# One column block of the output projection: the weights' low parts come from an adding DMA instead of a VectorE subtraction

## The chip, the cores and the metric

The kernel runs on one core of a Trainium2 chip. The core has five engines that work side by side, each through its own queue, in order: TensorE (PE in the profile; PEld is its weight load), VectorE (DVE), ScalarE (ACT), GpSimd (POOL) and SyncE (SP). Sixteen DMA engines move data between the chip's memory (HBM), where inputs and outputs lie, and the on-chip memory. A DMA is started by an instruction in the queue of SP, ACT or POOL. The metric is the device time of one execution in microseconds (us), smaller is better. Before the change it is 1098.4 us (median of three runs, 1097.79 to 1098.97).

## The reference

One layer of a decoder trunk on 512 tokens of width 2048. The change touches the output projection, the third line here:

```python
h = rms_norm(x, norm_g[i])
z = jnp.einsum('btd,dn->btn', h, w_in[i])        # then two head groups, gated, give y_mix
x = x + jnp.einsum('btc,cd->btd', y_mix, w_out[i])
gate = jax.nn.sigmoid(jnp.einsum('btd,de->bte', x, w_pg[i]) + b_pg[i])
x = x + gate * jnp.einsum('btq,qd->btd', p[i], w_ple[i])
return rms_norm(x, final_g)
```

`y_mix` is 512 x 2048 and `w_out` 2048 x 2048, all float32.

## The kernel before, in words

TensorE multiplies in the type float32r, which keeps fewer bits than float32. To keep the precision each operand is split into a high part (the value cast to float32r) and a low part (the value less the high part, cast too), and each product is made of three: high by high, high by low, low by high. `mm3` (L164) issues these three matmuls into one PSUM tile.

The program runs in stages: the input projection with the recurrence over the heads beside it (to about 728 us), the output projection (728 to 909 us), the gate projection and the final norm. The output projection goes through four column blocks of 512 columns, `ec` = 0 to 3 (loop at L987). In a block `proj` (L940) goes through 16 chunks of 128 rows of `w_out`, in the order 8 to 13, 0 to 7, 14, 15 (`order`). A chunk is a tile of 128 x 512 float32, 256 KB. For each chunk, and each of the four token tiles `tt`, `mm3` runs once: 12 matmuls of 128x512 a chunk, into four accumulators `acc_o`. The first matmul of a token tile reads `whi`, the second `wlo`, the third `whi` again (with `ylo`).

A chunk is prepared by `wsplit` (L127):

```python
raw = wp.tile([P, kt, n], F32, name=f"raw_{nm}", tag="raw")
nc.sync.dma_start(out=raw, in_=src)
hi = wp.tile([P, kt, n], F32R, name=f"whi_{nm}", tag="whi")
lo = wp.tile([P, kt, n], F32R, name=f"wlo_{nm}", tag="wlo")
nc.scalar.copy(hi, raw)
nc.vector.tensor_tensor(lo, raw, hi.bitcast(F32), ALU.subtract)
```

So SP starts the load of `raw`, ACT casts it to `whi` (L132), DVE subtracts to `wlo` (L133). The tags `raw`, `whi` and `wlo` have four buffers each (`wp`, `bufs=4`). ACT can cast a chunk only when TensorE has done with the chunk four places before it, whose buffer it takes; the loads run further ahead.

At the end of a block DVE adds `x` to each accumulator (L995), ACT's queue starts a store of the sum to `x2d` (L996) and later a load of the next block's `x` (L994). TensorE transposes the sums in 16 pieces of 128 x 128 (L1002) into four tiles `px`, each of which ACT casts to `x2hi` and DVE splits to `x2lo` (L137, L138). The framework's scheduler sets the order of the instructions on each engine from its own estimate of their times; no order is written out by hand in this stage. POOL has no work in the stage, and no instruction in the whole program that starts a DMA.

Of the kernel before, what the change touches and what calls it, by code (L numbers as in the profile page):

```python
# [9 lines left out]
F32 = mybir.dt.float32  # L10
F32R = mybir.dt.float32r
I32 = mybir.dt.int32
AF = mybir.ActivationFunctionType
ALU = mybir.AluOpType

P = 128
# [18 lines left out]
def trunk_kernel(ctx: ExitStack, tc: tile.TileContext, x, p, norm_g, w_in, mu, w0, w_up, a0, a_up,  # L35
                 k_k, k_a, r_k, ln_w, ln_b, w_pool, pool_scale, w_out, w_ple, w_pg, b_pg, final_g, out):
    nc = tc.nc
    PSUM = bass.MemoryType.PSUM
    x, p, w_in, w_out, w_ple, w_pg = x[0], p[0, 0], w_in[0], w_out[0], w_ple[0], w_pg[0]
    out = out[0]  # L40
# [3 lines left out]
    wp = ctx.enter_context(tc.tile_pool(name="wp", bufs=4))  # L44
# [82 lines left out]
    def wsplit(src, kt, n, nm):  # L127
# [6 lines that stand above are left out]
        return hi, lo  # L134

    def split(hi, lo, src):
        c_ = nc.scalar.copy(hi, src)  # L137
        nc.vector.tensor_tensor(lo, src, hi.bitcast(F32), ALU.subtract)  # L138
        return c_
# [24 lines left out]
    def mm3(ps, wh, wl, xh, xl, first, last):  # L164
        mm(ps, wh, xh, start=first, stop=False)
        mm(ps, wh, xl, start=False, stop=False)
        return mm(ps, wl, xh, start=False, stop=last)
# [8 lines left out]
    def chunk(nm, c, ahead=2):  # L176
        while (nm, c) not in ready or ahead > 0:
            if (nm, c) in ready:
                ahead -= 1
            if not plan:  # L180
                break
            n_, c_, src, kt, w_ = plan.pop(0)
            if (n_, c_) not in ready:
                ready[n_, c_] = wsplit(src, kt, w_, f"{n_}_{c_}")
        return ready.pop((nm, c))
# [8 lines left out]
    EC = 512  # L194
# [101 lines left out]
    for d in range(KT):  # L296
        xt_half(0, d)
        if d in WPOS:
            c = len(wl_)
            wh = wp.tile([P, CK, P], F32R, name=f"whi_l_{c}", tag="whi")  # L300
            wl = wp.tile([P, CK, P], F32R, name=f"wlo_l_{c}", tag="wlo")
# [586 lines left out]
    for j in range(NJ):  # L888
# [6 lines left out]
        if j + 1 == NJ:  # L895
            pn.append(rw.tile([P, NT, DPLE], F32, name="pn", tag="ar", bufs=2))
            for h in range(2):
                nc.scalar.dma_start(out=pn[0][:, 2 * h:2 * h + 2, :],
                                    in_=p[256 * h:256 * h + 256, :].rearrange("(t p) q -> p t q", p=P))
# [16 lines left out]
    def load_y(k):  # L916
        t_ = ymp.tile([P, T], F32, name=f"yin{k}", tag="yin", bufs=AHEAD)
        nc.scalar.dma_start(out=t_, in_=yd[k])
        split(yhi[:, k, :], ylo[:, k, :], t_)
# [15 lines left out]
    def acc_tile(nm):  # L935
        nacc[0] += 1
        pool, tag = (psB, "accb") if nacc[0] % 5 in (1, 2, 3) else (psA, "acc")
        return pool.tile([P, EC], F32, name=nm, tag=tag)

    def proj(w, hi_, lo_, ec, nm, ks=range(KT), tts=range(NT), keep=None, aside=None):  # L940
        acc = {tt: acc_tile(f"acc_{nm}{ec}_{tt}") for tt in tts}
        for i, k in enumerate(ks):
            src = w[k * P:(k + 1) * P, ec * EC:(ec + 1) * EC].unsqueeze(1)
            if nm == "o" and ec == 0 and i + AHEAD < KT:
                load_y(ks[i + AHEAD])
            if (f"{nm}{ec}_{k}", 0) in ready:
                wh, wl = ready.pop((f"{nm}{ec}_{k}", 0))
            elif nm == "o" and ec == 0 and i < 4:
                wh, wl = chunk(f"{nm}{ec}_{k}", 0)
            elif keep is None or LATE <= i < KT - KEEP:  # L950
                wh, wl = wsplit(src, 1, EC, f"{nm}{ec}_{k}")
            else:
                raw = wp.tile([P, 1, EC], F32, name=f"raw_{nm}{ec}_{k}", tag="raw")
                nc.sync.dma_start(out=raw, in_=src)
                if i < 2:
                    if i == 0:
                        two = [pp.tile([P, 2, EC], F32R, name=f"{g}k", tag=g, bufs=1) for g in ("dh", "dl")]
                    wh, wl = (g[:, i:i + 1, :] for g in two)
                else:
                    own = i < KT - 4  # L960
                    wh, wl = ((kp_ if own else wp).tile([P, 1, EC], F32R, name=f"{g}k{k}",
                                                        tag=f"{g}k{k}" if own else g) for g in ("whi", "wlo"))
                split(wh, wl, raw)
                keep[k] = (wh, wl)
                if i >= LATE:
                    continue
            for tt in tts if keep is None or i >= LATE else tts[:-1]:
                ts_ = slice(tt * P, (tt + 1) * P)
                first = i == (LATE if keep is not None and tt == NT - 1 else 0)
                e_ = mm3(acc[tt], hi_[:, k, ts_], lo_[:, k, ts_], wh[:, 0, :], wl[:, 0, :], first, i == KT - 1)  # L970
            if aside is not None and i == 2:
                with tc.issue_after(e_.ins):
                    hi = aside()
                with tc.issue_after(hi.ins):
                    recall(0, lp)
        return acc
# [3 lines left out]
    def recall(ec, pool):  # L980
        ples[ec] = []
        for tt in range(NT):
            t_ = pool.tile([P, EC], F32, name=f"pler{ec}_{tt}", tag="ple", bufs=4)
            nc.scalar.dma_start(out=t_, in_=pled[tt * P:(tt + 1) * P, ec * EC:(ec + 1) * EC])
            ples[ec].append(t_)

    for ec in range(D // EC):  # L987
        es = slice(ec * EC, (ec + 1) * EC)
        acc = proj(w_out, yhi, ylo, ec, "o", order)
        x2 = []  # L990
        for tt in range(NT):
            rows = slice(tt * P, (tt + 1) * P)
            t_ = pp.tile([P, EC], F32, name=f"x2_{ec}_{tt}", tag=("u", "sw")[tt // 2])
            nc.scalar.dma_start(out=t_, in_=x[rows, es])  # L994
            nc.vector.tensor_tensor(t_, acc[tt], t_, ALU.add)  # L995
            nc.scalar.dma_start(out=x2d[rows, es], in_=t_)  # L996
            x2.append(t_)
        def turn(ec=ec, x2=x2):
            for i in range(EC // P):
                pt = psM.tile([P, T], F32, name=f"px2_{ec}_{i}", tag="m")  # L1000
                for tt in range(NT):
                    nc.tensor.transpose(pt[:, tt * P:(tt + 1) * P], x2[tt][:, i * P:(i + 1) * P], ident)  # L1002
                hi = split(x2hi[:, 4 * ec + i, :], x2lo[:, 4 * ec + i, :], pt)
            return hi


        if ec < D // EC - 1:
            turn()
# [4 lines left out]
    with tc.tile_pool(name="fp", bufs=2) as fp, tc.tile_pool(name="kp_", bufs=1) as kp_:  # L1013
# [92 lines left out]
        for ec in range(LAST):  # L1106
            pre = {}
            vec = vectors(ec)
            acc = proj(w_pg, x2hi, x2lo, ec, "g", aside=turn if ec == 0 else None)
            ple = ples.pop(ec)  # L1110
            recall(ec + 1, fp if ec % 2 == 0 else lp)
            for tt in range(NT):
                fetch(ec, tt)
                gate(acc[tt], ec, tt, slice(ec * EC, (ec + 1) * EC), ec)
        ec = LAST
# [3 lines left out]
        for tt in range(NT):  # L1119
            fetch(ec, tt)  # L1120
        acc = proj(w_pg, x2hi, x2lo, ec, "g", keep=kept)


# [57 lines left out]
```

## Time and profile before

| | |
|---|---|
| median of three runs | 1098.4 us (1097.79 to 1098.97) |
| profiled execution | 1097.72 us |
| its span, first to last instruction | 1095.9 us |
| mean granted TensorE clock | 0.998 |
| second column block of the output projection | 772.57 to 817.99 us: 45.42 us |
| third column block | 817.99 to 863.44 us: 45.45 us |

The span is what the profiler saw between the first and the last instruction; the device time is 1.8 us longer. A timeline row gives the start, the duration, the engine, the line, the tiles written and read, and in brackets how long the engine had idled and for whom. ACTq and SPq rows are the instructions with which a queue starts DMAs, not the transfers. Matmuls overlap in the pipeline, so the distance between starts is the pace, and the duration is not. A strip of DMA digits shows the busy share of the 16 DMA engines in tenths, in 40 equal slices of the stretch asked for.

### The profile page before, as it was taken

To read this page: it belongs to the slowest core of one execution; us is meant where nothing else is said; L and a number is where in the kernel's file an instruction comes from. 1 tells how busy PE (TensorE), PEld (TensorE's weight loads), DVE (VectorE), ACT (ScalarE), POOL (GpSimd) and SP (SyncE) were. 2 spreads that over 40 slices of the span, in tenths; PEclk is the share of its full clock that TensorE was granted. 3 is DMA by queue.
4 is the path that set the end of the run, shared out by engine and by line. 5 is a ranking of instruction groups with operands and counts; after the bars stand their busy time and mean duration, and the time that the engine had idled before them with its cause. 6 is when DMAs were issued, how large, how long until landed. Compare 5 with 4: busy or idle time off the path is not lost.

```text
span 1095.9 us, 17196 instructions
## 1 busy us (share of the span) xinstructions
PE 1070.8 (98%) x6060; PEld 877.6 (80%) x6060; DVE 708.2 (65%) x1835; ACT 448.3 (41%) x917; POOL 76.9 (7%) x180
## 2 busy tenths in 40 slices
PE   5999999999999999999999999999999999999996
PEld 4888878887788888788878788888888888888885
DVE  6687867878688679678886956454433424445366
ACT  7633535345335335353343344543222222233337
POOL 2100110110110110100101101000000000000000
PEclk9999999999999999999999999999999999999999
DMA  7433433332423333333334242775534438455534
GB/s 233 116 96 97 111 92 84 96 100 73 120 82 105 104 92 89 96 82 93 91 94 119 79 138 93 232 233 169 172 124 136 167 99 244 137 189 137 181 106 154
DMA packets 178486, 138.56 MB, mean 126 GB/s; under 512 B 34678, under 2 KB 139743, under 8 KB 178399
## 3 DMA queue, kind: packets, MB, share of 16 engines
q1 hardware_dynamic: 157694, 103.89, 32.1%
q10 hardware_dynamic: 20704, 33.56, 9.8%
q8 instruction: 48, 0.79, 0.3%
q14 instruction: 40, 0.32, 0.1%
HBM read 118.02 MB, written 18.87 MB: 125 GB/s over the span
## 4 chain that ended last, share of the span: by engine, by line
PE 86%; DVE 5%; DMA 4%; ACT 3%; issue 1%; SPq 0%; ACTq 0%; DVEq 0%
PE acc_o L157 16%; PE zb L157 14%; PE acc_g L157 14%; PE zv L157 8%; PE zk L157 7%; PE zg L157 7%; PE zr L157 7%; PE py L157 2%; PE pple L157 2%; PE pm L157 1%; PE pu L157 1%; DMA n<-nd 1%; PE pp L157 1%; DMA raw_g<-in_w_pg_dram 1%; PE ps L157 1%
## 5 line engine op out<-in xcount | busy, mean ns | idle before, releaser
L133 DVE TENSOR_TENSOR wlo_g<-raw_g,whi_g 128x512 fp32r<-128x512 f32 x84 | 57.0, 685 | 79.6 <-ACT whi_g L132 76.5
L157 PE MATMUL zb<-hhi,whi_b 128*128 128x512 f32 x256 | 107.0, 418 | 0.0
L133 DVE TENSOR_TENSOR wlo_o<-raw_o,whi_o 128x512 fp32r<-128x512 f32 x64 | 43.9, 690 | 91.4 <-ACT whi_o L132 91.4
L157 PE MATMUL zb<-hhi,wlo_b 128*128 128x512 f32 x256 | 100.5, 393 | 0.0
L157 PE MATMUL acc_o<-whi_o,ylo 128*128 128x512 f32 x256 | 100.2, 391 | 0.0
L157 PE MATMUL acc_o<-whi_o,yhi 128*128 128x512 f32 x256 | 99.9, 390 | 0.0
L157 PE MATMUL zb<-hlo,whi_b 128*128 128x512 f32 x256 | 99.9, 390 | 0.0
L157 PE MATMUL acc_o<-wlo_o,yhi 128*128 128x512 f32 x256 | 99.8, 390 | 0.0
L132 ACT CAST whi_g<-raw_g 128x512 fp32r<-128x512 f32 x84 | 51.9, 620 | 102.7 <-PE acc_g L157 55.4
L157 PE MATMUL acc_g<-whi_g,x2hi 128*128 128x512 f32 x208 | 81.3, 391 | 0.0
L157 PE MATMUL acc_g<-wlo_g,x2hi 128*128 128x512 f32 x208 | 80.9, 389 | 0.0
L157 PE MATMUL acc_g<-whi_g,x2lo 128*128 128x512 f32 x208 | 80.7, 389 | 0.0
L132 ACT CAST whi_o<-raw_o 128x512 fp32r<-128x512 f32 x64 | 39.9, 623 | 97.0 <-PE acc_o L157 96.7
L816 POOL TENSOR_SCALAR s0p<-sbd,pw 64x64 f32<-64x64 f32 x96 | 56.6, 589 | 322.8 <-DVE sbd L809 255.0
L132 ACT CAST whi_b<-raw_b 128x512 fp32r<-128x512 f32 x64 | 39.7, 621 | 86.5 <-PE zv L157 35.4
L133 DVE TENSOR_TENSOR wlo_b<-raw_b,whi_b 128x512 fp32r<-128x512 f32 x64 | 43.8, 685 | 34.2 <-ACT whi_b L132 32.9
L157 PEld LDWEIGHTS zb<-hhi,wlo_b 128*128 128x128 f32 x256 | 48.0, 188 | 11.1
L661 DVE TENSOR_TENSOR xw<-xw,tm 128x60 f32<-128x60 f32 (+24 forms) x248 | 52.1, 210 | 6.8
L157 PEld LDWEIGHTS acc_o<-wlo_o,yhi 128*128 128x128 f32 x256 | 48.1, 188 | 10.3 <-DVE wlo_o L133 0.4
L157 PEld LDWEIGHTS acc_o<-whi_o,yhi 128*128 128x128 f32 x256 | 48.1, 188 | 9.7
L157 PEld LDWEIGHTS acc_o<-whi_o,ylo 128*128 128x128 f32 x256 | 48.1, 188 | 9.8
L157 PEld LDWEIGHTS zb<-hhi,whi_b 128*128 128x128 f32 x256 | 48.2, 188 | 8.5
(285 smaller groups left out, 2550.0 us busy)
## 6 DMA issues: line engine op xcount, KB each, us to landing
raw_b<-in_w_in_dram SPq DMA_DIRECT2D x64, 256.0 KB
raw_o<-in_w_out_dram SPq DMA_DIRECT2D x64, 256.0 KB
raw_g<-in_w_pg_dram SPq DMA_DIRECT2D x64, 256.0 KB
raw_k<-in_w_in_dram SPq DMA_DIRECT2D x32, 256.0 KB
raw_r<-in_w_in_dram SPq DMA_DIRECT2D x32, 256.0 KB
raw_v<-in_w_in_dram SPq DMA_DIRECT2D x32, 256.0 KB
raw_g<-in_w_in_dram SPq DMA_DIRECT2D x32, 256.0 KB
n<-nd SPq DMA_DIRECT2D x16, 256.0 KB
```

What stands on the lines that cost most here:

```text
L132: nc.scalar.copy(hi, raw)
L133: nc.vector.tensor_tensor(lo, raw, hi.bitcast(F32), ALU.subtract)
L157: i = nc.tensor.matmul(*a, **k)
L661: nc.vector.tensor_tensor(xw[:, 0:n_, s + 1:32], xw[:, 0:n_, s + 1:32], tm[:, 0:n_, 0:w_], ALU.add)
L816: nc.gpsimd.tensor_scalar(s0p[hc, :], nxt[hc, hc], pcn[hc], None, ALU.mult)
```

## The change

In the second column block alone (`ec == 1`, all 16 chunks) the chunk is prepared in another way. SP still loads `raw` and ACT still casts it to `whi`. Then ACT writes the negated high part to `wlo`, and a DMA in POOL's queue reads the same piece of `w_out` from HBM a second time and adds it onto `wlo`. DVE has no part in it.

```diff
@@ -947,6 +947,14 @@
             elif nm == "o" and ec == 0 and i < 4:
                 wh, wl = chunk(f"{nm}{ec}_{k}", 0)
+            elif nm == "o" and ec == 1:
+                raw = wp.tile([P, 1, EC], F32, name=f"raw_{nm}{ec}_{k}", tag="raw")
+                nc.sync.dma_start(out=raw, in_=src)
+                wh = wp.tile([P, 1, EC], F32R, name=f"whi_{nm}{ec}_{k}", tag="whi")
+                wl = wp.tile([P, 1, EC], F32R, name=f"wlo_{nm}{ec}_{k}", tag="wlo")
+                nc.scalar.copy(wh, raw)
+                nc.scalar.activation(wl, wh.bitcast(F32), AF.Copy, scale=-1.0)
+                nc.gpsimd.dma_start(out=wl, in_=src, accum_op=ALU.add)
             elif keep is None or LATE <= i < KT - KEEP:
                 wh, wl = wsplit(src, 1, EC, f"{nm}{ec}_{k}")
```

DVE loses 16 instructions, ACT gains 16 and POOL gains 16. Lines after L949 move down by 8, so the transposes of L1002 stand at L1010 in the rows of the changed kernel. The scheduler also orders TensorE's and ACT's instructions otherwise at the seam of the first and the second block.

On TensorE, at the seam before the change: `px_0_i` is the transpose of the first block's column piece i, `x_0_tt` the sum of token tile tt, `acc_o_0_8485` the second block's first accumulator.

```order
L1002 MATMUL px_0_0_8457<-ident,x_0_2_8449 128x128
L1002 MATMUL px_0_1_8464<-ident,x_0_2_8449 128x128
L1002 MATMUL px_0_2_8471<-ident,x_0_2_8449 128x128
L157 MATMUL acc_o_0_8485<-whi_o_8_8491,yhi 128x512
L157 MATMUL acc_o_0_8485<-wlo_o_8_8492,yhi 128x512
L1002 MATMUL px_0_0_8457<-ident,x_0_3_8453 128x128
L1002 MATMUL px_0_1_8464<-ident,x_0_3_8453 128x128
L1002 MATMUL px_0_2_8471<-ident,x_0_3_8453 128x128
L157 MATMUL acc_o_0_8485<-whi_o_8_8491,ylo 128x512
```

The same place on TensorE in the changed kernel:

```order
L1010 MATMUL px_0_2_8471<-ident,x_0_0_8441 128x128
L1010 MATMUL px_0_2_8471<-ident,x_0_1_8445 128x128
L1010 MATMUL px_0_0_8457<-ident,x_0_3_8453 128x128
L1010 MATMUL px_0_1_8464<-ident,x_0_3_8453 128x128
L1010 MATMUL px_0_2_8471<-ident,x_0_2_8449 128x128
L1010 MATMUL px_0_2_8471<-ident,x_0_3_8453 128x128
L157 MATMUL acc_o_0_8485<-whi_o_8_8491,yhi 128x512
L157 MATMUL acc_o_0_8485<-wlo_o_8_8492,yhi 128x512
L157 MATMUL acc_o_0_8485<-whi_o_8_8491,ylo 128x512
```

The three transposes of the last token tile now stand ahead of the block's first matmuls, and the four transposes of `px_0_3` stand two matmuls earlier than before (ahead of the fourth token tile's first matmul, not of its third).

On ACT, at the same seam before the change (chunks 11 and 12 are the fourth and fifth of the block; `x_1_tt` are the loads of the second block's `x`):

```order
L137 CAST x2hi<-px_0_2_8471 128x512
L132 CAST whi_o_11_8545<-raw_o_11_8543 128x512
L137 CAST x2hi<-px_0_3_8478 128x512
L132 CAST whi_o_12_8563<-raw_o_12_8561 128x512
L994 DMA x_1_0_8777<-in_x_dram 128x512
L994 DMA x_1_1_8781<-in_x_dram 128x512
L994 DMA x_1_2_8785<-in_x_dram 128x512
L132 CAST whi_o_13_8581<-raw_o_13_8579 128x512
```

The same place on ACT in the changed kernel:

```order
L137 CAST x2hi<-px_0_2_8471 128x512
L955 CAST whi_o_11_8548<-raw_o_11_8546 128x512
L1002 DMA x_1_0_8793<-in_x_dram 128x512
L137 CAST x2hi<-px_0_3_8478 128x512
L956 ACTIVATE wlo_o_11_8549<-whi_o_11_8548 128x512
L955 CAST whi_o_12_8567<-raw_o_12_8565 128x512
L1002 DMA x_1_1_8797<-in_x_dram 128x512
L956 ACTIVATE wlo_o_12_8568<-whi_o_12_8567 128x512
L955 CAST whi_o_13_8586<-raw_o_13_8584 128x512
L1002 DMA x_1_2_8801<-in_x_dram 128x512
```

The negation of chunk 11 stands behind the cast of `px_0_3`, not directly behind its own cast; from chunk 12 on the negation follows its cast, with at most the start of one load between. The four loads of `x` are spread over chunks 11 to 13.

On POOL the 16 new DMA instructions (L957) follow each other in the order of the chunks, each behind a wait for ACT's negation. On DVE the 16 subtractions are gone and nothing else moves; SP issues the same loads in the same order, each now released by ACT's cast of the buffer's last user in place of DVE's subtraction.

## Rows read from the trace of the kernel before

**Rows 1.** The page's first part: busy time, share of the span, instructions.

```profile
PE 1070.8 (98%) x6060; PEld 877.6 (80%) x6060; DVE 708.2 (65%) x1835; ACT 448.3 (41%) x917; POOL 76.9 (7%) x180
```

**Rows 2.** Busy time by stretch: the second and the third block.

```profile
core 0: us, PE busy (x) PEld busy (x) DVE busy (x) ACT busy (x) POOL busy (x), PEclk, DMA share, GB/s
772.57:817.99 45.42, 45.42 (x209) 37.59 (x208) 15.84 (x26) 11.91 (x20) 0.00 (x0) 1.00 0.42 139
817.99:863.44 45.45, 45.45 (x209) 37.59 (x208) 15.86 (x26) 11.91 (x20) 0.00 (x0) 1.00 0.43 139
```

**Rows 3.** Waits in 773 to 819 us: total, times, longest.

```profile
ACT whi_o L132 <- PE acc_o L157: 29.1, 14, 2.1
DVE wlo_o L133 <- ACT whi_o L132: 27.5, 14, 2.0
...
PEld px L1002 <- DVE x L995: 0.2, 1, 0.2
```

**Rows 4.** Timeline of one steady chunk in the second block.

```profile
785.15 0.39 PE L157 MATMUL acc_o<-whi_o,ylo 128*128 128x512 f32 x1
785.38 0.39 PE L157 MATMUL acc_o<-whi_o,yhi 128*128 128x512 f32 x1
...
785.62 0.62 ACT L132 CAST whi_o<-raw_o 128x512 fp32r<-128x512 f32 x1 [2.09 <-PE acc_o L157]
...
786.27 0.69 DVE L133 TENSOR_TENSOR wlo_o<-raw_o,whi_o 128x512 fp32r<-128x512 f32 x1 [2.02 <-ACT whi_o L132]
...
793.76 0.39 PE L157 MATMUL acc_o<-wlo_o,yhi 128*128 128x512 f32 x1
```

**Rows 5.** Costliest groups on ACT, shapes apart: an activation of a 128x512 tile.

```profile
L1061 ACT ACTIVATE x2r<-gt 128x512 f32<-128x512 f32 x15 | 9.4, 626 | 5.3 <-DVE gt L1056 5.3
```

**Rows 6.** Costliest groups on POOL: its most frequent instruction.

```profile
L816 POOL TENSOR_SCALAR s0p<-sbd,pw 64x64 f32<-64x64 f32 x96 | 56.6, 589 | 322.8 <-DVE sbd L809 255.0 <-DVE sbd L807 63.3
```

**Rows 7.** Timeline of the seam between the first and the second block.

```profile
770.71 0.69 DVE L133 TENSOR_TENSOR wlo_o<-raw_o,whi_o 128x512 fp32r<-128x512 f32 x1 [2.03 <-ACT whi_o L132]
...
771.32 2.48 DVE L995 TENSOR_TENSOR x<-acc_o,x 128x512 f32<-128x512 f32 x4
...
772.34 0.39 PE L157 MATMUL acc_o<-whi_o,ylo 128*128 128x512 f32 x1
...
772.57 1.22 PE L1002 MATMUL px<-ident,x 128*128 128x128 f32 x9
...
773.55 0.47 PE L157 MATMUL acc_o<-whi_o,yhi 128*128 128x512 f32 x1
...
774.11 0.49 PE L1002 MATMUL px<-ident,x 128*128 128x128 f32 x3
...
776.52 0.60 PE L1002 MATMUL px<-ident,x 128*128 128x128 f32 x4
...
777.15 0.59 ACT L137 CAST x2hi<-px 128x512 fp32r<-128x512 f32 x1 [0.66 <-PE px L1002]
...
782.88 0.39 PE L157 MATMUL acc_o<-wlo_o,yhi 128*128 128x512 f32 x1
```

**Rows 8.** SP's timeline, 786.9 to 790 us: two loads of `raw_o` start.

```profile
787.00 3.00 SPq L129 DMA_DIRECT2D raw_o<-in_w_out_dram  x2
```

**Rows 9.** DMA strip of 786.8 to 790.8 us, a digit per 0.1 us.

```profile
DMA  1000000000086367778663411110000000000003
```

**Rows 10.** DMA queue of SP, 788.9 to 816.1 us (ten loads): packets, MB, share.

```profile
q1 hardware_dynamic: 1440, 2.63, 30.2%
```

**Rows 11.** DMA queues in 777 to 783 us; q10 is ACT's, q1 is SP's.

```profile
q10 hardware_dynamic: 467, 0.85, 42.2%
q1 hardware_dynamic: 257, 0.48, 23.1%
```

**Rows 12.** SP's timeline, 136 to 152 us: the slowest 256 KB loads start.

```profile
141.29 1.15 SPq L644 DMA_DIRECT2D n<-nd  x2
```

**Rows 13.** DVE's timeline, 140 to 150 us: the reader that waits for them.

```profile
147.90 0.19 DVE L657 TENSOR_TENSOR tm<-i,n 128x31 f32<-128x31 f32 x1 [2.33 <-DMA n<-nd]
```

## The prediction

> **What bounds the kernel now.** I read the page's engine shares first. TensorE is busy 98% of the span, DVE 65%, ACT 41%, POOL 7% [rows 1]. A share of the whole says little about one stage, so I read the busy times by stretch. In the second block TensorE is busy for all of its 45.42 us, at the full granted clock, while DVE has 15.84 us of work, ACT 11.91 and POOL none; the third block, which the change leaves alone, has the same numbers within 0.03 [rows 2]. Then the waits inside the stretch: ACT waits for TensorE 14 times, 29.1 us in all, DVE waits for ACT 27.5 us, and the only wait of TensorE on anyone is 0.2 us, once, at the seam [rows 3]. So the preparation of the weights runs behind TensorE, released by it, and DVE, which the change relieves, holds up nothing. The reader should see a loop of four buffers: TensorE ends a chunk, ACT casts into the buffer it frees, DVE subtracts, and TensorE comes to that buffer three chunks later. The price of a longer preparation is set by the room in this loop.
>
> **The room.** The last matmul of a chunk starts at 785.15 and lasts 0.39; ACT's cast begins at 785.62; the next chunk has begun at 785.38. The matmul at 793.76 is the second one of the chunk that uses this buffer, the first to read `wlo` [rows 4]. From the start of the cast to that matmul are 793.76 - 785.62 = 8.14 us. A chunk takes (793.76 - 785.38 - 0.23) / 3 = 2.72 us, with 0.23 between two matmuls' starts (785.15 to 785.38). Today cast and subtraction end at 786.27 + 0.69 = 786.96, which leaves 6.8 us unused.
>
> **The change part by part.**
>
> *Removed:* 16 subtractions of 0.69 us, 11.0 us of DVE. Nothing on the path: TensorE does not wait for them. Worth 0, except at the seam (below).
>
> *Added on ACT:* 16 negations. The nearest row is an activation of a 128x512 tile in on-chip memory, 0.626 us [rows 5]; 16 x 0.63 = 10 us. ACT has 11.91 us of work in 45.42, so it stays under half busy, and the cost is latency alone. Room left when the DMA may start: 8.14 - 0.62 (cast) - 0.63 (negation) - two handovers of 0.03 (cast end 786.24 to DVE's 786.27 [rows 4]) = 6.8 us.
>
> *Added on POOL:* 16 DMAs, each from ACT's semaphore to the landing of 256 KB added onto `wlo`. Behind a waiting one stand only the other DMAs of the same kind, POOL has nothing else here; who waits for it is TensorE, which takes its matmuls in order, so the whole stage stands when one is late. The trace shows no DMA from POOL and no adding one. I call its time L and bound it. Below: a plain load of the same 256 KB starts at 787.00 [rows 8], its packets run from slice 11 to about slice 27 of the strip, 787.9 to 789.5 [rows 9]: 2.6 us, of which 1.7 are transfer. Above: the slowest 256 KB load in the trace, in small pieces, started at 141.29 [rows 12] and its reader began at 147.90 after waiting for it [rows 13]: 6.6 us, plus one POOL instruction of 0.59 [rows 6] for writing the transfer's list, 7.2. I take the plain load, which moves the same rows to the same tile, with its transfer paid twice (an add must read `wlo` as well as `w_out`) and the POOL instruction: 2.6 + 1.7 + 0.6 = 4.9 us. That is under 6.8, so in the steady part the DMA is hidden and costs nothing; the cover is TensorE's three chunks.
>
> The Trainium skill, DMA: Bandwidth & Descriptors (Anatomy of one DMA), gives a DMA issued from GpSimd a fixed 2.0 us plus its bytes at 436 GB/s, as an estimate 2.6 us for 256 KB; the plain load's row has the same 2.6, from another queue. Collectives: The Full Stack (the bandwidth ceiling) says that an adding transfer runs at half rate because of two source reads, not because of the add, so the estimate would be 3.2 us; no row here shows an adding one. By 3.2 every chunk would be in time and the sum would be 0.1 us.
>
> *Moved at the seam, TensorE:* the block's start has 12 transposes first, where two matmuls stood between to bridge DVE's last add. DVE's four adds begin at 771.32, 0.6 apart, because `wlo` of the third chunk runs from 770.71 [rows 7]; that subtraction is gone, so the last add waits only for its accumulator, closed at 772.34 + 0.39 = 772.73, and ends near 773.5 instead of 773.8. TensorE starts the transposes at 772.57, 0.109 apart (nine until 773.55), and needs the last add after eight, at 773.44. It waits about 0.1 us. Bounds: 0.4 if the adds come as late as now, -0.16 if the present 0.2 wait goes. I take +0.1.
>
> *Moved at the seam, ACT:* the fourth chunk (11) is the tight one. Its negation stands behind the cast of `px_0_3`. The four transposes of `px_0_3` start at 776.52 now; two matmuls (0.45) go behind them, so with the 0.1 they start near 776.2. The cast followed by 0.63 us (776.52 to 777.15) and took 0.59, so it ends near 777.4, the negation near 778.0, and POOL can start at 778.05. The second matmul of chunk 11 is the one at 782.88 [rows 7], then 782.98. The room is 4.9 us, no more than L. For chunk 12 the cast and the negation follow, to about 779.3, and its matmul is 2.72 later, at 785.7: 6.4 us.
>
> *DMA engines:* a load takes 30.2% of 27.2 us in ten, 0.82 us of all sixteen engines [rows 10]; an adding one, read twice, 1.64. Per chunk of 2.72 us: 0.82 + 1.64 = 2.46, 90% in the steady part. From 777 to 783 ACT's and SP's loads take 42.2% and 23.1% [rows 11], and the adds of chunks 11 and 12 would bring 2 x 1.64 / 6 = 55% on top: 120%. So the transfer of chunk 11 is drawn out, and I charge it one load that goes first, 0.8 us. It is then late by 4.9 + 0.8 - 4.9 = 0.8 us. Chunk 12 has 1.5 us more room and is in time.
>
> *SP's loads* are released by ACT's cast, one subtraction sooner; they run ahead and gain nothing.
>
> *Sum:* 0 (DVE) + 0 (ACT) + 0.1 (seam) + 0.8 (chunk 11) = +0.9 us, in a profiled execution of 1097.7 (span 1095.9 and 1.8 around it). That one lies 0.7 below the median; on the median of 1098.4 the forecast is 1099.3. A change of under 0.2%, 2.2 us, can't be told from none here.
>
> **Rivals.**
>
> *The loop of four buffers becomes the bound (slower).* Place: the wait of each chunk's second matmul. Once L passes 6.8, chunk 11 is late by L - 4.9 and its buffer's later users (the 8th, 12th and 16th chunk) by L - 6.8 each; the others are covered by these delays. Price: 4L - 25.3. It passes 2.2 us from L = 6.9. At the upper bound 7.2 it is 3.5, with the seam 3.6: 1102.0. For it: the upper row, and an operation and a queue that no row shows. Against it: the plain load's 2.6, and L must be nearly three times that.
>
> *The DMA engines become the bound (slower).* If an add costs three loads (read, read, write), 2.46 + 0.82 = 3.28 us are wanted per 2.72: 0.56 for 12 chunks, 6.7 us, 1105.2 with the seam. For it: 90% already by my count, and loads of the next block in the same queues. Against it: a load also reads and writes, and is 0.82 in all.
>
> *DVE's relief shows (faster).* If the seam's 0.2 us wait goes and TensorE changes once less between transposes and matmuls (0.1 us at most), about 0.3 us are won: 1098.1. More than that would need TensorE's pace to hang on DVE, and the pace is the same in both blocks and through stretches where DVE idles. To pass 0.2% it would need seven times the wait that is there.
>
> **How the numbers follow.** Forecast (hidden but for the seam and chunk 11, up to 2.2 us) 66%; buffers 20%, DMA engines 10%; DVE's relief, to an extent that shows, 4%. So slower 0.30, same 0.66, faster 0.04. The range goes down to the gain at the seam less the spread of the runs (1098.1 - 0.6, about 1097.6) and up to the DMA engines' case with that spread, 1106; beyond it remain adds slower than any row. The forecast's own range is 1098.0 to 1100.6.
>
> **What would show it.** In the changed profile: ACT rows of L956 at 0.63; TensorE waiting for a DMA onto `wlo_o` once, near 783 us, under 2 us; 16 starts at L957 with 256 KB, each landing in about 5; the second block at 46.3 us and the third still at 45.45. Wrong would be: repeated waits of TensorE every fourth chunk (the loop), a strip full of nines through the block with `raw_o` late (the DMA engines), or a second block shorter than 45.2 us (DVE mattered).

## The result, and the profile after

Over 13 runs of each, the changed kernel takes 1101.08 us at the median (1098.85 to 1104.13) and the kernel before 1098.23 (1096.60 to 1099.60): ratio 1.0027, interval 1.0017 to 1.0037. It is slower by 2.9 us at the median. The prediction took 0.2% as the least that can be told from no change; the median lies just above it, and the interval reaches just below. The profiled execution, 1102.82 us with a span of 1101.1, is among the slowest of the 13, so the losses read from it below add up to more than the median's.

Busy time by stretch, the second and the third block (before: [rows 2]):

```profile
core 0: us, PE busy (x) PEld busy (x) DVE busy (x) ACT busy (x) POOL busy (x), PEclk, DMA share, GB/s
773.74:824.40 50.66, 47.40 (x210) 38.73 (x208) 6.72 (x12) 20.01 (x33) 11.22 (x13) 0.97 0.83 196
824.40:869.85 45.45, 45.45 (x209) 37.60 (x208) 15.86 (x26) 11.91 (x20) 0.00 (x0) 1.00 0.41 140
```

The third block is unchanged to 0.01 us. The second, from its first transpose to that of the next, is 5.21 us longer than the 45.45 of before (772.57 to 818.02). TensorE stands 3.26 us in it, and its granted clock is 0.97 on average. The DMA share has doubled from 0.42. (The view counts a packet's whole time where the packet starts, so a short stretch can show a share above 1.)

The waits in 766 to 820 us (engine and line, what for, total, times, longest; before: [rows 3]):

```profile
ACT whi_o L955 <- PE acc_o L157: 25.0, 14, 6.6
...
PE acc_o L157 <- DMA wlo_o<-in_w_out_dram: 3.3, 1, 3.3
```

TensorE waits for an adding DMA once. On TensorE's timeline (start, duration, idle before):

```profile
783.85 0.39 PE L157 MATMUL acc_o<-whi_o,yhi 128*128 128x512 f32 x1
787.50 0.50 PE L157 MATMUL acc_o<-wlo_o,yhi 128*128 128x512 f32 x1 [3.26 <-DMA wlo_o<-in_w_out_dram]
...
788.36 0.63 PE L157 MATMUL acc_o<-wlo_o,yhi 128*128 128x512 f32 x1
788.79 0.63 PE L157 MATMUL acc_o<-whi_o,ylo 128*128 128x512 f32 x1
```

It is the second matmul of the fourth chunk (11), the place that the prediction named. It starts 787.50 - 783.85 - 0.23 = 3.42 us late. Behind it the matmuls last 0.63 and stand 0.43 apart in place of 0.39 and 0.23: TensorE runs at 1.2 GHz, the lower of its two levels. The same by stretch (the column before the DMA share is the granted clock):

```profile
787.50:788.50 1.00, 1.00 (x4) 0.81 (x5) 0.00 (x0) 0.00 (x0) 0.00 (x0) 0.88 1.09 295
788.50:789.50 1.00, 1.00 (x4) 0.81 (x3) 0.00 (x0) 0.00 (x0) 0.00 (x0) 0.50 1.12 291
...
791.50:792.50 1.00, 1.00 (x6) 0.81 (x5) 0.00 (x0) 0.57 (x1) 0.00 (x0) 0.91 0.74 137
```

The twelve steps from 787.50 to 791.97 take 4.47 us in place of 12 x 0.227 = 2.72, a second loss of 1.75 us. Of it 0.11 is the first step, 0.34 in place of 0.23; a step like it stands behind the waits without a lower clock too (0.34 in the first experiment below). The rest is the clock's. 3.42 + 1.75 = 5.17 of the 5.21.

The other end of the wait, in the chain of waits:

```profile
779.36 0.01 POOLq L957
779.38 8.08 DMA wlo_o<-in_w_out_dram
```

ACT's negation ended at 778.45 + 0.63 = 779.08, POOL began its DMA 0.3 us later, and the add landed 8.08 us after that. What the adds are as a group (durations in ns, minimum, median and maximum; then landing in us; then the page's row of their queue):

```profile
L956 ACT ACTIVATE wlo_o<-whi_o x16: 629/632/634, 766.4 to 814.4; 128x512 fp32r<-128x512 f32 x16
L957 POOL DMA_DIRECT2D wlo_o<-in_w_out_dram x16: 862/862/1027, 767.4 to 815.3; - x16
...
DMA to landing us min/median/max: 3.9/4.6/9.4
```

```profile
q0 software_dynamic: 2304, 4.20, 2.3%
```

An add occupies the sixteen engines for 0.023 x 1101.1 / 16 = 1.58 us, nearly twice a load's 0.82 [rows 10]. Landings fall into two groups. Looked at one by one, the adds that start at 767.38 and 770.09 and the nine from 793.51 on land in 3.9 to 4.7 us; the five from 772.80 to 785.62 take 7.1, 8.1, 9.0, 9.4 and 8.0. That is the stretch in which ACT's queue carries the first block's four stores to x2d and the second block's four loads of x. The 8.1 us of the late add fall into two parts (q10 is ACT's queue, q0 the adds, q1 SP's loads). From 779.38 to 783.00 there is no packet of q0 at all:

```profile
q10 hardware_dynamic: 175, 0.32, 39.2%
q1 hardware_dynamic: 160, 0.29, 34.1%
```

From 783.00 to 787.46:

```profile
q0 software_dynamic: 219, 0.41, 54.3%
q10 hardware_dynamic: 258, 0.48, 30.0%
q1 hardware_dynamic: 165, 0.31, 20.1%
```

In the second part the engines are full (the shares add up to 104%). In the first they are 73% busy, and the add still moves nothing for 3.6 us. An add behind the seam, issued at 793.51, also has no packet until 795.00:

```profile
q1 hardware_dynamic: 140, 0.26, 56.6%
```

That is 1.5 us. So of the 3.5 us by which the late add exceeds the median landing some 2.1 pass before its first packet, on engines that are not full, and 1.4 after it. What holds the packets back is not shown. The stretch behind the seam, without q10:

```profile
793.50:818.00 24.50, 24.50 (x109) 20.30 (x109) 0.69 (x1) 10.67 (x17) 7.76 (x9) 1.00 0.88 189
```

0.88 is (1.58 + 0.82) / 2.72, what a chunk asks of the engines. In that state everything is hidden. It leaves 12% free for anything else.

### The profile page after: what moved, and what is told of

It reads as the page before. It is cut to its first block, busy times and chain, and to the rows that moved or that the text cites. A ratio compares the mean times of both kernels' runs of the same rounds, so it can differ in the third digit from the quotient of the medians.

```text
span 1101.1 us, 17233 instructions
## 1 busy us (share of the span) xinstructions
PE 1072.7 (97%) x6060; PEld 879.0 (80%) x6060; DVE 698.1 (63%) x1819; ACT 458.5 (42%) x933; POOL 90.4 (8%) x196
## 4 chain that ended last, share of the span: by engine, by line
PE 83%; DMA 5%; DVE 5%; ACT 3%; issue 2%; SPq 0%; ACTq 0%; DVEq 0%; POOLq 0%
PE acc_g L157 16%; PE acc_o L157 15%; PE zb L157 14%; PE zv L157 7%; PE zr L157 6%; PE zg L157 6%; PE zk L157 5%; DMA n<-nd 2%; PE py L157 2%; PE pple L157 2%; PE pm L157 1%; PE pu L157 1%; PE pp L157 1%; PE ps L157 1%; DMA wlo_o<-in_w_out_dram 1%
## 5 line engine op out<-in xcount | busy, mean ns | idle before, releaser
L133 DVE TENSOR_TENSOR wlo_o<-raw_o,whi_o 128x512 fp32r<-128x512 f32 x48 | 32.8, 690 | 98.5 <-ACT whi_o L132 98.5
L132 ACT CAST whi_o<-raw_o 128x512 fp32r<-128x512 f32 x48 | 29.8, 623 | 65.9 <-PE acc_o L157 65.6
```

## The experiments

The question was which of three things makes the add late: where the fourth chunk stands in ACT's and POOL's order, what else the DMA engines carry, or the operation itself; and what lowers the clock. All ratios are against runs of the kernel before on the same chip (medians 1096.45, 1096.90 and 1096.73 us in the three groups of four). The diffs are cut to the lines that carry the experiment.

**Adds only from the fifth chunk on.**

```diff
-            elif nm == "o" and ec == 1:
+            elif nm == "o" and ec == 1 and i >= 4:
```

> The first four chunks of the second block (8, 9, 10, 11) are split by DVE again, the other twelve keep the negation and the adding DMA. Theory (one late add: the fourth chunk's, whose start stands behind the cast of px_0_3 and whose transfer meets the seam's stores and loads; TensorE stands 3.4 us and then runs 3.6 us at half clock): the cost goes, the ratio to before is 1.000 within 0.001, the second block takes 45.4 to 45.8 us and TensorE waits for no add. Rival, the steady part costs (buffers or DMA engines, twelve of sixteen adds are left): the ratio stays at 1.002 to 1.003.

Ratio 1.0024 [1.0015, 1.0033], not the 1.000 expected. The fifth and the sixth chunk are late in place of the fourth:

```profile
786.83 0.50 PE L157 MATMUL acc_o<-wlo_o,yhi 128*128 128x512 f32 x1 [0.59 <-DMA wlo_o<-in_w_out_dram]
790.50 0.50 PE L157 MATMUL acc_o<-wlo_o,yhi 128*128 128x512 f32 x1 [0.64 <-DMA wlo_o<-in_w_out_dram]
```

Their adds take 7.1 and 8.3 us. The block is 47.31 long (+1.86), at full clock. So the fourth chunk's late start is not the whole cause: the adds next to it, with more room, are slow and late too.

**An add for the fourth chunk alone.**

```diff
+            elif nm == "o" and ec == 1 and i == 3:
```

> Only the fourth chunk (11) takes the adding DMA, the other fifteen are split by DVE. Theory of the late fourth add: TensorE still waits for it, once. The other adds' traffic is gone (chunks 9, 10 and 12 are DVE's), so its landing should take 5 to 6.5 us in place of 8.1, against a room of 4.7: a wait of 0.3 to 1.8 us, +0.5 to +2.5 us in all with the clock, ratio 1.0005 to 1.002. Rival, the sum of the sixteen adds' traffic is the cause: no wait, ratio 1.000.

Ratio 1.0036 [1.0023, 1.0049], above the 1.002 expected at most. One add without any other still takes 6.9 us, over the 5 to 6.5 expected, and TensorE stands for it:

```profile
785.83 0.60 PE L157 MATMUL acc_o<-wlo_o,yhi 128*128 128x512 f32 x1 [2.45 <-DMA wlo_o<-in_w_out_dram]
```

So a single add pays as much as sixteen, within the intervals: the steady load of the other fifteen is not needed for the loss. Nor were the engines full while it flew, 0.79 busy on average in its 6.9 us.

Behind this wait the clock falls too. Just before and just after the fall (last three numbers: granted clock, DMA share, GB/s):

```profile
785.50:786.08 0.58, 0.25 (x1) 0.25 (x2) 0.00 (x0) 0.00 (x0) 0.00 (x0) 1.00 0.95 357
786.08:786.50 0.42, 0.42 (x2) 0.31 (x2) 0.00 (x0) 0.00 (x0) 0.00 (x0) 0.50 0.96 356
```

The adds of the other chunks are not needed for the fall. But the DMA engines were busy when it came, so this run does not part the wait from the traffic.

**The fourth chunk's cast, negation and DMA put ahead.**

```diff
+                with tc.high_priority(offset=EARLY if i == 3 else 0):
                     nc.scalar.copy(wh, raw)
                     nc.scalar.activation(wl, wh.bitcast(F32), AF.Copy, scale=-1.0)
                     nc.gpsimd.dma_start(out=wl, in_=src, accum_op=ALU.add)
```

> All sixteen adds stay, but the fourth chunk's cast, negation and add are given a higher priority, so that on ACT they stand ahead of the four casts of px. The add starts some 4 us sooner, so the room grows from 4.7 to over 8 us. The fifth chunk's negation moves behind the cast of px_0_3, which leaves it about 6 us. Theory: the fourth chunk is in time; if the fifth lands within 6 us the cost is gone (ratio 1.000 to 1.0005), if the seam's traffic draws it to 8 us there is a wait of up to 2 us there. Rival, traffic alone decides and not the start: the same wait as in the changed kernel, ratio 1.0027.

Ratio 1.0012 [1.0003, 1.0021]: lower than the change's 1.0027, though the intervals touch, and not free. The fourth chunk is in time (DMA at 776.46, landing 8.1 us later); the fifth, landing after 7.4, is late:

```profile
788.90 0.50 PE L157 MATMUL acc_o<-wlo_o,yhi 128*128 128x512 f32 x1 [0.97 <-DMA wlo_o<-in_w_out_dram]
```

**ACT negates, VectorE adds.** No adding DMA; ACT's negations stay as in the change.

```diff
-                nc.gpsimd.dma_start(out=wl, in_=src, accum_op=ALU.add)
+                nc.vector.tensor_tensor(wl, raw, wl.bitcast(F32), ALU.add)
```

> ACT negates as in the changed kernel and the order of ACT and TensorE at the seam is the changed one, but DVE adds raw to the negated part; no DMA from POOL. Theory: nothing is late, ratio 1.000 within 0.001, second block 45.4 to 45.7 us. Rival, ACT's sixteen negations or the new order at the seam make part of the cost: ratio above 1.001 with a wait of TensorE on ACT or DVE.

Ratio 0.9996 [0.9988, 1.0005], and the block is back at its length with ACT at 20.03 us:

```profile
773.75:819.21 45.46, 45.46 (x210) 37.61 (x208) 16.03 (x26) 20.03 (x33) 0.00 (x0) 1.00 0.42 138
```

ACT's negations cost nothing. TensorE's order at the seam was meant to stay as in the change, but did not: six transposes, not twelve, stand before the block's first matmul. That the change's own order costs next to nothing is seen in its own profile (0.03 us, below) and in the run with thirteen adds, which has this order and no loss. What is left for the loss is the DMA.

**The four loads of x later**, behind ACT's negation of the tenth chunk.

```diff
+            if ec == 1:
+                with tc.issue_after(behind_[0].ins):
+                    nc.scalar.dma_start(out=t_, in_=x[rows, es])
```

> As the changed kernel, but the four loads of x for the second block (1 MB on ACT's queue) are issued only behind ACT's negation of the tenth chunk, about 12 us later than now; the stores of the first block's x2d (1 MB on the same queue) stay at the seam. Theory (an add takes about 4.4 us beside the weight loads alone and 6.3 to 9.4 us while transfers of ACT's queue flow, and a chunk is late where that is more than its room of 4.7 us for the fourth and about 6.4 for the others): the adds of the fourth to seventh chunk land in 4.4 to 6.5 us in place of 8.1, 9.0, 9.4 and 8.0; TensorE waits for the fourth chunk at most 1.8 us in place of 3.3, the granted clock stays at 1.00 behind it, and the ratio is 1.000 to 1.0012. The adds that now meet the loads of x (tenth chunk and its neighbours) get longer, to 6 to 8 us, and may cost one wait under 1.5 us. Rival (the adds are slow at the seam because of SP's weight loads and the other adds, or because the seam's loads catch up): landings stay at 8 to 9 us there, the wait stays near 3.3 us with half a clock behind it, ratio 1.0027.

Ratio 1.0035 [1.0022, 1.0048]; 1.0012 at most was expected. The fourth chunk's wait shrinks as expected (with the four stores alone the seam's adds still take 5.6 to 7.6 us), but the adds that now meet the loads of x land in 7.5 to 8.7 us, and two waits are added:

```profile
784.77 0.50 PE L157 MATMUL acc_o<-wlo_o,yhi 128*128 128x512 f32 x1 [1.40 <-DMA wlo_o<-in_w_out_dram]
802.16 0.50 PE L157 MATMUL acc_o<-wlo_o,yhi 128*128 128x512 f32 x1 [0.75 <-DMA wlo_o<-in_w_out_dram]
805.74 0.50 PE L157 MATMUL acc_o<-wlo_o,yhi 128*128 128x512 f32 x1 [0.57 <-DMA wlo_o<-in_w_out_dram]
```

The cost has moved with the loads. The theory's place was right and its price wrong: four loads in a row, 3.3 us of the engines, find 0.32 us free per chunk (2.72 - 2.40).

**The same, and the first block's stores left out.**

```diff
+            if ec > 0:
                 nc.scalar.dma_start(out=x2d[rows, es], in_=t_)
```

> As the run with the late loads of x, and besides the first block's four stores to x2d are left out (the gate then reads the second block's columns in their place, so that the output is not the reference's): at the seam nothing flows but the weight loads and the adds. Theory: the adds of the fourth to seventh chunk land in 4.0 to 5.0 us; the fourth chunk, with its room of 4.7 us, is late by at most 0.5 us, no other at the seam; no half clock; ratio 0.9995 to 1.0006, apart from what the moved loads of x do later (one wait under 1.5 us at most). Rival (not the transfers of ACT's queue, but the weight loads and the adds themselves): landings of 7 us and more there still, a wait of 2 to 3.4 us, ratio 1.002 to 1.0027. If the stores alone were to blame, this run would be quick and the run with the late loads of x not.

Ratio 1.0022 [1.0013, 1.0031], from waits of 1.16 and 0.34 us where the loads of x now are; at the seam there is none. The trace shows the two states side by side, first 772 to 791 us, without ACT's queue (last number: median landing in us):

```profile
wlo_o<-in_w_out_dram POOLq DMA_DIRECT2D x7, 256.0 KB, 4.7
```

then 792 to 802, with it:

```profile
q0 software_dynamic: 377, 0.70, 42.9%
q10 hardware_dynamic: 565, 1.03, 33.0%
q1 hardware_dynamic: 367, 0.68, 21.9%
...
wlo_o<-in_w_out_dram POOLq DMA_DIRECT2D x4, 256.0 KB, 7.8
```

The three queues together fill 98% of the engines. An add is slow where transfers of ACT's queue flow, wherever in the block that is. The rival, that adds and weight loads alone make it slow, falls.

**The same DMA without the adding.**

```diff
-                nc.gpsimd.dma_start(out=wl, in_=src, accum_op=ALU.add)
+                nc.gpsimd.dma_start(out=wl, in_=src)
```

> As the changed kernel, but the DMA from GpSimd writes the weights over the negated high parts in place of adding onto them (so the low parts are the whole weights, and the output is not the reference's): same issue, same bytes from HBM, no reading of the target. Theory (the add takes 1.58 us of the sixteen engines because it reads twice, against 0.82 of a load): the queue's share falls from 2.3% of the span to about 1.2%, the landing without other transfers from 4.4 us to about 3, at the seam from 8 to 9 us to 5 to 6; the fourth chunk is late by 0.3 to 1.3 us, no half clock, ratio 1.0003 to 1.0012. Rival (the price is that of a GpSimd-issued DMA as such, its list and its descriptors, not of the adding): share 2.3% and landings of 4.4 and 8 to 9 us as with the add, ratio 1.0027.

Ratio 1.0016 [1.0007, 1.0025], a little over what was expected. The profiled run, 1097.02 us, is among the fastest of its eleven: its block takes 45.97 us with one wait of 0.19, so no trace shows where the median's 1.8 us go. The page's row of the queue, and its landing in the quiet stretch of 787 to 810 us:

```profile
q0 software_dynamic: 2304, 4.20, 1.4%
```

```profile
wlo_o<-in_w_out_dram POOLq DMA_DIRECT2D x9, 256.0 KB, 3.4
```

1.4% is 0.96 us of the engines. So the adding costs 1.58 - 0.96 = 0.62 of them and about 1 us of landing (3.4 against 4.4); at the seam this DMA lands in 4.6 to 6.0 us where the add takes 8.0 to 9.4. The adding makes the landings longer at the seam; that it also raises the kernel's time is likely but not clear, since this interval and the change's (1.0017 to 1.0037) overlap.

**Own buffers for the fourth to sixth chunk.**

```diff
+                own = 3 <= i < 6
+                wh, wl = ((ymp if own else wp).tile([P, 1, EC], F32R, name=f"{g}_{nm}{ec}_{k}",
+                                                    tag=f"{g}{i}" if own else g, bufs=1 if own else None)
+                          for g in ("whi", "wlo"))
```

> As the changed kernel, but the fourth, fifth and sixth chunk have buffers of their own for their high and low parts, so that ACT makes and negates them before the seam's casts and their adds start up to 10 us earlier; every transfer stays. Theory (lateness is landing time less room): the adds at the seam still take 6 to 9 us each where the transfers of ACT's queue flow, but TensorE waits for none of them by more than 0.5 us, because the room of the fourth to ninth chunk is 10 us and more; no half clock; second block 45.5 to 46 us, ratio 0.9996 to 1.0006. Rival (the transfers' load on the engines itself slows TensorE or delays the weight loads, whatever the room): a loss of 1 us and more stays, ratio 1.001 to 1.0027, with waits on raw or on the low parts further down the block.

Ratio 1.0062 [1.0049, 1.0074]: my expectation fell. The earlier starts put adds of the fourth to sixth chunk beside the four stores, and the third chunk's add, now issued last of six, takes 10 us (from the chain of waits):

```profile
774.70 10.06 DMA wlo_o<-in_w_out_dram
```

```profile
784.81 0.55 PE L157 MATMUL acc_o<-wlo_o,yhi 128*128 128x512 f32 x1 [3.90 <-DMA wlo_o<-in_w_out_dram]
```

The DMA share is 1.03 and 1.09 in the two halves of 770 to 782 us. Counted from the block's first transpose, the third chunk's add starts 3.0 us later than in the change (774.70 against 772.65, and 772.80 against 773.74) and lands 3.0 us slower (10.06 against 7.08). So half of its lateness is its new place in the queue and half the slower landing: room given to some chunks was taken from another. That, and the late loads of x, turned "a transfer of ACT's queue in flight makes an add slow" into a sum, which the next two runs try: what the engines are asked in a stretch, against the stretch.

**VectorE for the fourth to sixth chunk, adds for the other thirteen.**

```diff
-            elif nm == "o" and ec == 1:
+            elif nm == "o" and ec == 1 and not 3 <= i < 6:
```

> As the changed kernel, but the low parts of the fourth, fifth and sixth chunk come from VectorE again; the other thirteen stay adding DMAs. Theory (the sixteen DMA engines have 2.72 us per chunk and are asked for 1.58 for an add and 0.82 for a load, 88%; only beside the seam's eight transfers of x2d and x, 0.82 each, is more asked than there is, and only adds started there land later than their room): no TensorE wait on a low part over 0.5 us, landings of 4 to 5 us from the eighth chunk on, the seventh at most 6.5; second block 45.4 to 46 us, granted clock 1.00; ratio 0.9995 to 1.0006. Rival (adding DMAs cost TensorE something wherever they are, by traffic or by wakeups): thirteen of sixteen remain, ratio 1.0015 to 1.0027.

Ratio 1.0003 [0.9994, 1.0012], no wait of TensorE on a low part, and the block at 45.48 us:

```profile
772.78:818.26 45.48, 45.48 (x210) 37.66 (x208) 8.69 (x15) 18.34 (x30) 8.63 (x10) 1.00 0.79 202
```

Thirteen of sixteen adds are free. With the three at the seam the loss is gone.

**All sixteen adds, the transfers spread.** The early fourth chunk, and the four loads of x one by one:

```diff
+                with tc.issue_after(behind_[(7, 9, 11, 13)[tt]].ins):
                     nc.scalar.dma_start(out=t_, in_=x[rows, es])
```

> All sixteen adds stay, with two mends: the fourth chunk's cast, negation and DMA go ahead of the seam's casts, as in the run with the early fourth chunk, and the second block's four loads of x are issued one by one behind the negations of the 8th, 10th, 12th and 14th chunk in place of all at the seam. Theory (DMA engines' time per chunk: 1.58 + 0.82, and 0.41 more where a load of x comes every second chunk, 2.81 against 2.72 us, so that the backlog grows by only some 0.1 us per chunk; at the seam only the four stores are left, 3.3 us, and the fourth chunk has 6.5 us and more of room): no wait of TensorE on a low part over 0.7 us, no half clock, second block 45.5 to 46.5 us, ratio 0.9997 to 1.0010. Rival (any transfer of ACT's queue in flight slows an add to 7 us and more, whatever the sum): four or more waits of about 0.6 us, ratio 1.002 and more.

Ratio 1.0004 [0.9995, 1.0013]: the adds and the bytes are all there, and no loss clear of the noise is left. TensorE waits once, for 0.18 us. The profiled block is 0.84 us longer than before; that wait and one smaller delay, with the slow steps next to them, make some 0.7 of it.

```profile
772.86:819.15 46.29, 46.10 (x209) 37.43 (x208) 6.72 (x12) 20.11 (x33) 11.21 (x13) 1.00 0.88 215
```

The share is 0.88 for the whole block (0.83 in the change: the same work, spread over a longer block). Landings outside the stores reach 7.2 us where the loads of x pass, and are hidden there. It is as fast as the kernel before, not faster. Two things were changed at once, and the early fourth chunk alone gave 1.0012 [1.0003, 1.0021]; what the spreading adds to it is not clear of the noise in the times, only in the waits (0.97 us there, 0.18 here).

The middle of this run also bears on the clock:

```profile
790.00:805.00 15.00, 15.00 (x66) 12.05 (x65) 0.00 (x0) 6.27 (x10) 5.18 (x6) 1.00 1.01 234
```

Fifteen us of full DMA engines, and TensorE, which does not stand, keeps the full clock. Traffic alone did not lower it.

**A stall without adds.** The kernel before, with two reciprocals on VectorE between cast and subtraction of the fourth chunk.

```diff
+                nc.vector.reciprocal(idle, wh.bitcast(F32))
+                slow = nc.vector.reciprocal(idle, wh.bitcast(F32))
```

> The kernel before, with no adding DMA at all; in the second block VectorE runs two reciprocals of a 128x512 tile (3.35 us each) into an unused tile between the cast and the subtraction of the fourth chunk, so that its low part is about 3 us late, as in the changed kernel. Theory (a wait of this length is by itself followed by a stretch at the lower granted clock, 1.2 GHz, that costs about 1.7 us): one wait of 2.6 to 3.4 us at the fourth chunk's second matmul, then 7 to 8 matmuls at half clock, second block 49.8 to 50.6 us, ratio 1.0036 to 1.0048. Rival (the clock falls because of the DMA traffic of the adds, not of the wait): the wait alone, clock 1.00 behind it, second block 48.3 to 48.9 us, ratio 1.0025 to 1.0032.

Ratio 1.0021 [1.0012, 1.0030]. The wait came out shorter than meant, and no lower clock follows it in the profiled execution (block 47.73 us):

```profile
785.89 0.50 PE L157 MATMUL acc_o<-wlo_o,yhi 128*128 128x512 f32 x1 [1.99 <-DVE wlo_o L960]
```

So this one does not decide by its profile. Its runs hint that a wait is enough, with no adds at all: 5 of 11 show a mean granted clock of 0.996 (median 1100.18 us), the other six 0.997 and 0.998 (1098.68); of the 27 runs of the kernel before beside it one shows 0.996. The changed kernel divides in the same way, seven runs at 0.996 (1102.01) and six above (1099.67).

**Adds in the second and the third block.**

```diff
-            elif nm == "o" and ec == 1:
+            elif nm == "o" and ec in (1, 2):
```

> The adding DMAs in the second and in the third block. Theory (each block pays at its first seam, where 88% of steady work meets the eight transfers): the third block's fourth chunk waits 3 us and more for its add as the second's does, with a stretch at half clock behind it where the wait is over 2 us; third block 48 to 51 us in place of 45.45, the sum twice that of one block, ratio 1.0045 to 1.0095. The steady stretch of the third block again without waits. Rival (a cost of the first use only, such as POOL's first DMA after 76 us of idleness): third block 45.5 us, ratio 1.0027.

Ratio 1.0067 [1.0053, 1.0081]. Each block has one wait at its fourth chunk, in the third just under the 3 us expected:

```profile
785.90 0.79 PE L157 MATMUL acc_o<-wlo_o,yhi 128*128 128x512 f32 x1 [2.27 <-DMA wlo_o<-in_w_out_dram]
...
836.22 0.50 PE L157 MATMUL acc_o<-wlo_o,yhi 128*128 128x512 f32 x1 [2.95 <-DMA wlo_o<-in_w_out_dram]
```

```profile
773.12:822.77 49.65, 47.38 (x209) 38.78 (x208) 5.32 (x9) 21.91 (x36) 13.80 (x16) 0.97 0.91 212
822.77:873.10 50.33, 47.38 (x209) 38.77 (x208) 6.72 (x12) 20.01 (x33) 11.22 (x13) 0.97 0.81 198
```

The price is paid per seam, 4.2 and 4.9 us in this execution, and is no matter of a first use.

## Why the prediction was right, and where its sizes were wrong

The time lies in the range and on the side of the sum (+0.9 forecast, +2.9 measured), but outside the forecast's own 1098.0 to 1100.6, the case that was given 66%. That the range holds it is partly luck: its upper part was there for a rival (an add that costs three loads, all through the block) that did not occur. The mechanism was right, a late add of the fourth chunk; its size was not.

- *VectorE's relief is worth nothing.* Right: 9.1 us less of it in the block (15.84 to 6.72), and no gain; nor with thirteen or sixteen adds whose waits are gone (1.0003 and 1.0004).
- *ACT's negations and the seam's order.* Negation 0.63 forecast, 0.632 measured. The order cost +0.03 of the +0.1: first transpose to the second chunk's start is 4.65 us, 4.62 before. The run with VectorE's add shows the negations at nothing, the run with thirteen adds the order.
- *The steady part is hidden.* Right: L was put at 4.9, and is 3.9 to 4.7 (the lower estimate beside the sum, 3.2, by which every chunk would be in time, was too low); an add was put at 1.64 us of the engines, and is 1.58; the share at 90%, and is 88%.
- *The fourth chunk is the tight one, with 4.9 us of room.* Right: 784.08 - 779.38 = 4.70 us. The missing 0.2 is in the main the handover from ACT to POOL, 0.30 where 0.05 was allowed.
- *The contention of the fourth chunk, 0.8 us.* This step failed. The prediction counted 120% of the engines asked in 777 to 783 us, and then charged one load that goes first. The add took 8.08 us, 3.5 more than the 4.6 median, where 0.8 was charged. The 120% were not asked in that stretch either: in the changed kernel its share is 0.82, with 7.7% for the adds, since the fourth chunk's add has no packet before 783. Then come full engines, 54% of them for four adds in flight. The late loads of x and the quiet seam show where the excess belongs: slow adds go where the transfers of ACT's queue go, and at the seam they vanish with them. How much is the sum of the engines' time and how much the late first packet is open; the single add, late at an average share of 0.79, suggests that a full sum is not needed.
- *"Chunk 12 has 1.5 us more room and is in time."* True in the change only because the fourth chunk's wait covers it. Without that cover it is late (0.59 and 0.97 us in the first and the third run).
- *Not in the sum at all: the clock.* Some 1.6 us in the profiled execution. That the fall follows the wait and not the traffic is likely, not shown: in the profiles it came only behind long waits, though the DMA engines were at 0.95 when it came in the run with one add; 1.01 for 15 us without a wait did not bring it; and some runs of the stall without adds have the lower mean clock. Waits of 2.27, 2.45, 2.95, 3.26 and 3.90 us were followed by it, waits of 1.99, 1.40, 1.16 and less were not. What decides it is left open, since the run made for it had too short a wait.
- *The rivals.* The loop of four buffers did not appear: no wait every fourth chunk. The DMA engines did hold the add back, but at the seam and not through the block, and not because an add costs three loads (1.58 us against 0.82 for one).

## What to carry to other kernels

When a change hands an engine's work to the DMA engines, add up their occupied time per period, and then look for the stretch with one-off transfers beside the steady ones. There even a single added DMA was late here, and whichever consumer is tightest pays. Moving the burst elsewhere moved the price; starting the tightest add earlier and spreading the burst, done together, took it away. And price a stall of TensorE with the lower clock that can follow it, here about half of the wait again.

## What the runs showed of the hardware

- An adding DMA issued from GpSimd: 0.86 us of POOL for each (1.03 for the first), 0.3 us from ACT's end to POOL's start, 1.58 us of the sixteen engines and 3.9 to 4.7 us to landing for 256 KB beside weight loads; up to 9.4 us in the change and 10.06 in the run with own buffers, where transfers of ACT's queue flow. The first packet came 1.5 us after the start in a quiet stretch and 3.6 us after it for the late add, at an engine share of 0.73. The same DMA without the adding: 0.53 us of POOL, 0.96 us, 3.3 to 3.8 us.
- The granted clock fell to 0.50 behind every wait of TensorE of 2.27 us and more in these profiles, and stayed at 1.00 through 15 us with the DMA engines at 1.01 and no wait.
